# Gated linear attention and retention: both heads of a tile issued side by side on TensorE

## The chip, the cores and the metric

The kernel runs on one core of one Trainium2 chip. The metric is the device time of one execution in microseconds: 3158.46 as the median of three runs (3155.77 to 3163.26).

## What is computed

Two transformer-like blocks run one after the other on a sequence of 512 tokens, width 1024, two layers each. The change lies in the second block. There each layer projects its input once, splits the projection among four mixers (HGRN, gated linear attention or GLA, RWKV-7, retention; 256 columns each, four heads each), joins them, projects again, normalises and runs a feed-forward part (dense in layer 0, eight experts in layer 1). The parts that matter, from the reference:

```python
def _chunked_gated_linear(q, k, v, log_f):          # HGRN and GLA
    def step(state, inp):
        ...
        scores = jnp.einsum('bhik,bhjk,bhijk->bhij', qi, ki, decay)
        out = (jnp.einsum('bhij,bhjv->bhiv', scores, vi)
               + jnp.einsum('bhik,bhkv->bhiv', qi * jnp.exp(cum), state))
        ...
def _retention_chunkwise(q, k, v, log_gamma):       # retention
    def step(state, inp):
        ...
        scores = jnp.einsum('bhik,bhjk->bhij', qi, ki) * intra
        out = (jnp.einsum('bhij,bhjv->bhiv', scores, vi)
               + jnp.einsum('bhik,bhkv->bhiv', qi * q_dec[..., None], state))
```

The kernel computes the same sums without the carried state, as masked products over all 512 tokens: a token looks at every earlier one with the decay between the two.

## The kernel before

Activations of the second block lie with features on the 128 partitions and the 512 tokens along the free axis. A tile of 128 partitions holds two heads of 64 values. Keys are 64 wide in HGRN and retention (two heads on a tile), 32 wide in GLA (four heads on a tile). Work is written as Python generators, one for each mixer core. `weave` runs several of them together: each `yield` gives a share of a stated total, and the one that is least far along is continued. What is traced in that order goes to a scheduler, which fixes the order of each engine's queue when the program is built: an instruction is queued when its inputs and its buffers are there by the scheduler's own clock, earlier traced ones first.

The end of `mixers` weaves three times per layer: the two RWKV pairs with the HGRN and GLA projections; then the two HGRN cores `H(0)` and `H(1)` with the retention projection; then the GLA core, the retention core and the first half (`ph1`) of the output projection. Nothing else changes around these stages.

`linear_core` is the HGRN core (`nh` = 2 heads of 64 rows, called twice) and the GLA core (`nh` = 4 heads of 32 rows, called once). It runs nine levels. In the first seven, TensorE makes scores of all heads into an `sc` bank (`sc<-lE,lxk`), and VectorE copies them under a mask into one table per head, `dg[h]` (`ldg` in the profile, line 1897). The last two levels leave `a` and `b` (`lqk`), which cover the pairs of different 128-token blocks. Then comes the part that the change rewrites (lines 1902 to 1923): for each pair `m` of heads and each head `u` of it, two score matmuls of 128 columns into an `sc` bank and a copy on ScalarE (line 1910, to `o2`), two of 256 columns into another `sc` bank and a copy (line 1914, to `o1`), and ten value matmuls (64 columns of values as weights, 128 tokens moving) into half of the bank `op` (tag `av`). Both copies are named `lof`. A head's keys are a slice of rows of the array, a head's values a slice of its columns.

`ret_core` does the four retention heads, two on each tile `i`. For a head it loads a decay table of 512 columns (`ret`, line 1964); then for each of four blocks of keys it makes the scores of 512, 384, 256 or 128 queries into an `sc` bank, multiplies them with the table on VectorE (line 1970, to `tmp`), and adds the product with the values to half of the bank `op`.

Float32 matmuls on these lines go through the helper `mm` (line 1521), so the profile shows all of them under L1521; the tiles tell them apart. Projections use three float32r matmuls for one product (lines 406 to 408) with 512 or 256 columns.

PSUM has eight banks of 512 float32 columns, two for each of the tags `mm`, `sc`, `tp` and `av`. SBUF tiles of 128 x 512 are taken from one pool, tag `C`, with 47 buffers; `tmp` has 6 of its own. All loads go through SP's queue in order.

Of the kernel before, what the change touches and what calls it, by code (L numbers as in the profile page):

```python
# [19 lines left out]
P = 128  # L20
D = 1024
S = 512
# [15 lines left out]
V = 1.2  # L38
# [276 lines left out]
class K:  # L315
# [88 lines left out]
    def mm3(self, out, lh, ll, rh, rl, first, last):  # L404
        mm = self.nc.tensor.matmul
        mm(out, lh, rh, start=first, stop=False)  # L406
        mm(out, lh, rl, start=False, stop=False)  # L407
        mm(out, ll, rh, start=False, stop=last)  # L408
# [1109 lines left out]
        return o  # L1518

    def mm(self, out, lhsT, rhs, start=True, stop=True):  # L1520
        self.nc.tensor.matmul(out, lhsT, rhs, start=start, stop=stop)  # L1521

    def sigmoid(self, out, ps, hb=None, n=P):
        nc = self.nc
# [298 lines left out]
    def linear_core(self, Q, Kk, Pf, nh, V, gs, gname, m0):  # L1823

        nc = self.nc
        kd = P // nh
        X = self.c("lx")
        nc.gpsimd.memset(X, 0.0)  # L1830
        q = lambda x, t: x[:, t * P:(t + 1) * P]
        bc4 = lambda m: m.unsqueeze(1).to_broadcast([P, 4, P])
        v4 = lambda x: x.rearrange("p (t c) -> p t c", c=P)
        rr = [slice(kd * h, kd * h + kd) for h in range(nh)]
        dg = self.cs(nh, "ldg")

        qk = self.c("lqk")
        nc.gpsimd.tensor_mul(qk, Q, Kk)
        dp = self.bank("sc")
        for t in range(4):  # L1840
            self.mm(dp[:, t * nh:(t + 1) * nh], q(qk, t), self.heads[nh])
        dc = self.xp.tile([P, 16], F32, name="ldc", tag="ldc", bufs=2)[:, :4 * nh]
        nc.scalar.copy(dc, dp[:, :4 * nh])
        dv = dc.rearrange("p (t h) -> p t h", h=nh)
        for h in range(nh):
            nc.gpsimd.tensor_mul(v4(dg[h]), bc4(self.ident), dv[:, :, h:h + 1].to_broadcast([P, 4, P]))
        yield 0.5

        xk = [self.c("lxk") for _ in range(2)]
        ng = nh // 2  # L1850
        E = [[self.c("lE") for _ in range(ng)] for _ in range(2)]
        for b in range(2):
            nc.gpsimd.memset(xk[b], 0.0)
            for g in range(ng):
                nc.gpsimd.memset(E[b][g], 0.0)
        nt = 4 // ng
        top = []
        for n in range(9):
            s = 1 << n
            lv = lambda x: x.rearrange("p (b s) -> p b s", s=2 * s)  # L1860
            e = self.c("le")
            x = self.c("lqk") if n > 6 else xk[n % 2]
            self.act(lv(e)[:, :, s:], lv(Pf)[:, :, s:], AF.Exp)
            self.act(lv(e)[:, :, :s], lv(X)[:, :, :s], AF.Exp)
            nc.vector.tensor_mul(lv(x)[:, :, :s], lv(Kk)[:, :, :s], lv(e)[:, :, :s])
            if n > 6:
                nc.vector.tensor_mul(lv(x)[:, :, s:], lv(Q)[:, :, s:], lv(e)[:, :, s:])
                top.append(x)
            else:
                for g in range(ng):  # L1870
                    ts = slice(g * nt * P, (g + 1) * nt * P)
                    ev = E[n % 2][g].rearrange("p (t h b s) -> p t h b s", h=nh, t=nt, s=s)
                    half = lambda y: y[:, ts].rearrange("p (t b s) -> p t b s", t=nt, s=2 * s)[:, :, :, s:]
                    if g in EA[nh]:
                        nc.vector.tensor_mul(half(e), half(Q), half(e))
                    for h in range(nh):
                        if g in EA[nh]:
                            self.act(ev[:, :, h], half(e), AF.Identity, scale=self.heads[nh][:, h:h + 1])
                        else:
                            nc.vector.tensor_mul(ev[rr[h], :, h], half(Q)[rr[h]], half(e)[rr[h]])  # L1880
            if n < 8:
                nb = S // (2 * s)
                pv, xv = lv(Pf), lv(X)
                nc.gpsimd.tensor_add(xv[:, :, :s], xv[:, :, :s], pv[:, :, 2 * s - 1:2 * s].to_broadcast([P, nb, s]))
                nc.gpsimd.tensor_add(pv[:, :, s:], pv[:, :, s:], pv[:, :, s - 1:s].to_broadcast([P, nb, s]))
            if n > 6:
                continue
            mask = self.lvt(n).rearrange("p (b s) -> p b s", s=2 * s)[:, :, s:].unsqueeze(1)
            for g in range(ng):
                ps = self.bank("sc")  # L1890
                w = 64 * nh
                for t in range(nt):
                    self.mm(ps[:, t * w:(t + 1) * w], q(x, g * nt + t), E[n % 2][g][:, t * w:(t + 1) * w])
                pv = ps.rearrange("p (t h b s) -> p t h b s", h=nh, t=nt, s=s)
                for h in range(nh):
                    dst = dg[h][:, g * nt * P:(g + 1) * nt * P]
                    nc.vector.copy_predicated(dst.rearrange("p (t b s) -> p t b s", t=nt, s=2 * s)[:, :, :, s:],
                                              mask.to_broadcast([P, nt, 64 // s, s]), pv[:, :, h])
                yield 0.9
        a, b = top  # L1900
        offs = {(0, 1): (1, 0), (0, 2): (0, 0), (0, 3): (0, 1), (1, 2): (0, 2), (1, 3): (0, 3), (2, 3): (1, 1)}
        for m in range(nh // 2):
            op = self.bank("av")
            for u in range(2):
                h = 2 * m + u
                o1, o2 = self.c("lof"), self.c("lof")
                ps = self.bank("sc")
                self.mm(ps[:, 0:128], q(a, 0)[rr[h]], q(a, 1)[rr[h]])
                self.mm(ps[:, 128:256], q(a, 2)[rr[h]], q(a, 3)[rr[h]])
                nc.scalar.copy(o2[:, 0:256], ps[:, 0:256])  # L1910
                ps = self.bank("sc")
                self.mm(ps[:, 0:256], q(b, 0)[rr[h]], b[rr[h], 256:512])
                self.mm(ps[:, 256:512], q(b, 1)[rr[h]], b[rr[h], 256:512])
                nc.scalar.copy(o1, ps)
                v, h0 = V[m]
                ov = slice(64 * u, 64 * u + 64)
                for t in range(4):
                    o = q(op, t)[ov]
                    for j in range(t):
                        w, f = offs[j, t]  # L1920
                        self.mm(o, v(j, 64 * (h0 + u), 64), q((o1, o2)[w], f), j == 0, False)
                    self.mm(o, v(t, 64 * (h0 + u), 64), q(dg[h], t), t == 0, True)
                yield 3.0
            sq = self.c("lsq")
            self.act(sq, op, AF.Square)
            vp = self.bank("tp")
            self.mm(vp, self.blk, sq)
            self.rsqrt(sq, vp, "m_rms")
            nc.vector.scalar_tensor_tensor(sq, op, self.v2(gname), sq, op0=ALU.mult, op1=ALU.mult)
            nc.vector.tensor_mul(sq, sq, gs[m])  # L1930
            self.emit_y(m0 + m, sq, 0.5)
            yield 0.9
# [24 lines left out]
    def ret_core(self, d):  # L1957
        nc = self.nc
        for i in range(2):
            op = self.bank("av")  # L1960
            for u in range(2):
                h = 2 * i + u
                rr = slice(64 * u, 64 * u + 64)
                tab = self.load(self.aps["cst2"][:, 1154 + S * h:1154 + S * (h + 1)], "ret")
                for t in range(4):
                    n = S - t * P
                    ps = self.bank("sc")
                    self.mm(ps[:, :n], d["k"][i][rr, t * P:(t + 1) * P], d["q"][i][rr, t * P:])
                    s = self.tmp()
                    nc.vector.tensor_mul(s[:, :n], ps[:, :n], tab[:, :n])  # L1970
                    self.mm(op[rr, t * P:], d["v"][0](t, 64 * h, 64), s[:, :n], t == 0, t == 3)
                    yield 1.0
            o = self.c("gn")
            nc.scalar.copy(o, op)
            n, rs = self.group_norm(o, "m_ln")
            nc.vector.tensor_mul(n, n, rs)
            nc.vector.tensor_mul(n, n, d["g"][i])
            self.emit_y(6 + i, n, 0.5)
            yield 1.8
# [22 lines left out]
```

## Time and profile before

| | |
|---|---|
| median of three runs | 3158.46 us |
| lowest, highest | 3155.77, 3163.26 us |
| the profiled execution | 3172.64 us, its span 3170.8 us |
| TensorE matmul busy | 3013.7 us (95% of the span) |
| TensorE weight loads | 2454.5 us (77%) |
| VectorE, ScalarE, GpSimd | 1889.4, 1316.5, 355.8 us (60%, 42%, 11%) |
| mean granted TensorE clock | 0.97 |

The profile is of one execution, taken by the hardware. PE is TensorE's matmuls, PEld its weight loads, which overlap them; DVE is VectorE, ACT ScalarE, POOL GpSimd, SP the queue that issues loads. `sc<-lqk 64*128 64x256` reads: written to a tile named `sc`, read from `lqk`, 64 rows by 128 columns of the array, moving data of 64 partitions by 256 columns. The end of a matmul is modelled and reaches into the next one, so what an instruction costs is read from start to start. The layers of the second block begin their weaves of the linear cores at about 1440 and 2274 us of the span.

### The profile page before, as it was taken

How to read it: one execution, taken by the hardware profiler on the slowest of the kernel's cores; microseconds unless marked ns; L12 is line 12 of the kernel's file. 1: busy time of each engine (PE TensorE's matmuls, PEld its weight loads, DVE VectorE, ACT ScalarE, POOL GpSimd, SP SyncE). 2: the span in 40 equal slices, each digit the busy share in tenths (PEclk: the TensorE clock that was granted, in tenths of full speed). 3: DMA queues.
4: the chain of work that ended last, by engine and by line, in shares of the span. 5: the costliest groups of instructions: out<-in, count | busy, mean ns of one | idle time of the engine just before them, and what ended most of it. 6: DMA issues, size and time to landing. Idle time of an engine off the chain costs nothing. (4 is left out here: it accounts for less than half of the span.)

```text
span 3170.8 us, 46930 instructions
## 1 busy us (share of the span) xinstructions
PE 3013.7 (95%) x18729; PEld 2454.5 (77%) x18729; DVE 1889.4 (60%) x3318; ACT 1316.5 (42%) x2257; POOL 355.8 (11%) x377
## 2 busy tenths in 40 slices
PE   7999999999999999998999999999999799999997
PEld 5688888877878888786657888778775599999983
DVE  6676554657745566636554333555556677777775
ACT  3534333335433333424333222343353366666652
POOL 2220000211100001004210000100222200000021
PEclk9999999999999999999999999999999899999997
DMA  5322124242221433210202323421112278777782
GB/s 181 105 79 80 61 66 146 84 146 77 74 87 47 136 103 111 72 42 24 90 21 94 98 95 94 133 89 42 34 47 81 80 235 264 261 251 258 248 282 93
DMA packets 116534, 365.69 MB, mean 115 GB/s; under 512 B 13584, under 2 KB 16784, under 8 KB 116304
## 3 DMA queue, kind: packets, MB, share of 16 engines
q1 hardware_dynamic: 113424, 353.13, 34.2%
q0 software_dynamic: 2880, 9.44, 0.9%
q8 instruction: 150, 2.46, 0.3%
q14 instruction: 80, 0.66, 0.1%
HBM read 344.83 MB, written 17.69 MB: 114 GB/s over the span
## 5 line engine op out<-in xcount | busy, mean ns | idle before, releaser
L399 DVE TENSOR_TENSOR wl<-wr,wh 128x1024 fp32r<-128x1024 f32 (+1 forms) x574 | 698.3, 1225 | 520.2 <-ACT wh L395 508.2
L395 ACT CAST wh<-wr 128x1024 fp32r<-128x1024 f32 (+1 forms) x574 | 594.3, 1045 | 744.2 <-PE mm L407 355.4
L406 PE MATMUL mm<-hh,wh 128*128 128x512 f32 (+1 forms) x1616 | 651.4, 403 | 0.2
L407 PE MATMUL mm<-hl,wh 128*128 128x512 f32 (+1 forms) x1616 | 646.6, 400 | 0.0
L408 PE MATMUL mm<-hh,wl 128*128 128x512 f32 (+1 forms) x1616 | 642.8, 398 | 2.0 <-DVE wl L399 2.0
L406 PEld LDWEIGHTS mm<-hh,wh 128*128 128x128 f32 (+1 forms) x1616 | 306.9, 190 | 73.9 <-issue 6.3
L408 PEld LDWEIGHTS mm<-hh,wl 128*128 128x128 f32 (+1 forms) x1616 | 306.0, 189 | 74.5 <-issue 4.7
L407 PEld LDWEIGHTS mm<-hl,wh 128*128 128x128 f32 (+1 forms) x1616 | 307.0, 190 | 69.8 <-issue 6.2
L1266 PE MATMUL mm<-xgT,wh 128*128 128x320 f32 x704 | 218.5, 310 | 0.0
L1266 PE MATMUL sc<-xgT,wh 128*128 128x320 f32 x704 | 218.2, 310 | 0.1
L1267 PE MATMUL mm<-xgT,wl 128*128 128x256 f32 x704 | 198.1, 281 | 3.5 <-DVE wl L399 3.5
L1267 PE MATMUL sc<-xgT,wl 128*128 128x256 f32 x704 | 197.9, 281 | 0.0
L1267 PEld LDWEIGHTS mm<-xgT,wl 128*128 128x128 f32 x704 | 133.3, 189 | 5.9 <-DVE wl L399 5.6
L1266 PEld LDWEIGHTS mm<-xgT,wh 128*128 128x128 f32 x704 | 132.6, 188 | 1.2 <-DVE xgT L1245 0.4
L1266 PEld LDWEIGHTS sc<-xgT,wh 128*128 128x128 f32 x704 | 132.8, 189 | 0.3 <-DVE tmp L1272 0.3
L1267 PEld LDWEIGHTS sc<-xgT,wl 128*128 128x128 f32 x704 | 132.7, 188 | 0.0
L439 POOL TENSOR_TENSOR rs<-rs,mhalf 128x1 f32<-128x1 f32 x36 | 29.7, 825 | 905.1 <-DVE rs L438 790.7
L406 PE MATMUL mm<-wh,hh 128*128 128x256 f32 x448 | 129.6, 289 | 0.6 <-DVE sgv L754 0.6
L408 PE MATMUL mm<-wh,hl 128*128 128x256 f32 x448 | 128.4, 287 | 0.0
L407 PE MATMUL mm<-wl,hh 128*128 128x256 f32 x448 | 128.4, 287 | 0.0
L728 DVE TENSOR_REDUCE mn<-sc 128x1 f32<-128x512 f32 x64 | 44.1, 689 | 86.1 <-PE sc L725 85.9
L1521 PE MATMUL sc<-lE,lxk 128*128 128x128 f32 (+1 forms) x336 | 65.3, 338 | 25.4 <-ACT lE L355 11.6
(552 smaller groups left out, 5741.2 us busy)
## 6 DMA issues: line engine op xcount, KB each, us to landing
wr<-mgu SPq DMA_DIRECT2D x176, 512.0 KB, 4.8
wr<-w SPq DMA_DIRECT2D x172, 512.0 KB, 3.7
wr<-md SPq DMA_DIRECT2D x88, 512.0 KB, 4.5
wr<-fgu SPq DMA_DIRECT2D x44, 512.0 KB, 3.7
wr<-wo SPq DMA_DIRECT2D x32, 512.0 KB, 3.8
wr<-wbr SPq DMA_DIRECT2D x24, 512.0 KB, 3.7
row<-rows SPq DMA_DIRECT2D x40, 256.0 KB, 5.4
wr<-fd SPq DMA_DIRECT2D x20, 512.0 KB, 3.6
```

What stands on the lines that cost most here:

```text
L395: nc.scalar.copy(hi[:, :n], raw[:, :n])
L399: nc.vector.tensor_sub(lo[:, :n], raw[:, :n], hi[:, :n].bitcast(F32))
L406: mm(out, lh, rh, start=first, stop=False)
L407: mm(out, lh, rl, start=False, stop=False)
L408: mm(out, ll, rh, start=False, stop=last)
L439: self.nc.gpsimd.tensor_tensor(out, out, self.mhalf, op=ALU.pow)
L728: nc.vector.tensor_reduce(mx[u][:, a:a + 1], sc, axis=AX.X, op=ALU.min)
L1266: mm(o[i][:, :2 * CAP], wh, x[:, k, :2 * CAP], start=k == 0, stop=False)
L1267: mm(o[i][:, :256], wl, x[:, k, :256], start=False, stop=k == KT - 1)
L1521: self.nc.tensor.matmul(out, lhsT, rhs, start=start, stop=stop)
```

## The change

A helper `turns` issues one matmul for each of the two heads in turn and ties every one after the first (by issue order, not by a wait) behind the first, which is that of head `u` = 1. `linear_core` now makes, for a pair of heads, the 128-column scores of both into the two `sc` banks in turns, copies both, makes the 256-column scores of both into the two `tp` banks in turns, copies both, and after a `yield` makes the values of both in turns into the two halves of one `av` bank. Per pair it uses four `lof` buffers. `ret_core` loads both tables of a tile first; `weigh(t)` makes the scores of both heads into both `sc` banks and multiplies both; the scores of step `t + 1` are issued ahead of the values of step `t`. The count of matmuls, copies, multiplications and loads is the same, and so are the totals of the `yield` shares. No constant changes.

```diff
--- before.py
+++ after.py
@@ -1518,7 +1518,17 @@
         return o
 
     def mm(self, out, lhsT, rhs, start=True, stop=True):
-        self.nc.tensor.matmul(out, lhsT, rhs, start=start, stop=stop)
+        return self.nc.tensor.matmul(out, lhsT, rhs, start=start, stop=stop)
+
+    def turns(self, f, xs):
+
+
+        first = None
+        for x in xs:
+            for u in (1, 0):
+                with self.tc.issue_after(first) if first else nullcontext():
+                    i = f(u, x)
+                first = first or i.ins
 
     def sigmoid(self, out, ps, hb=None, n=P):
         nc = self.nc
@@ -1900,27 +1910,29 @@
         a, b = top
         offs = {(0, 1): (1, 0), (0, 2): (0, 0), (0, 3): (0, 1), (1, 2): (0, 2), (1, 3): (0, 3), (2, 3): (1, 1)}
         for m in range(nh // 2):
+            rows = [rr[2 * m + u] for u in range(2)]
+            o1, o2 = self.cs(2, "lof"), self.cs(2, "lof")
+            ps = [self.bank("sc") for _ in range(2)]
+            self.turns(lambda u, z: self.mm(q(ps[u], z), q(a, 2 * z)[rows[u]], q(a, 2 * z + 1)[rows[u]]), range(2))
+            for u in (1, 0):
+                nc.scalar.copy(o2[u][:, 0:256], ps[u][:, 0:256])
+            pb = [self.bank("tp") for _ in range(2)]
+            self.turns(lambda u, z: self.mm(pb[u][:, 256 * z:256 * z + 256], q(b, z)[rows[u]], b[rows[u], 256:512]),
+                       range(2))
+            for u in (1, 0):
+                nc.scalar.copy(o1[u], pb[u])
+            yield 3.0
             op = self.bank("av")
-            for u in range(2):
-                h = 2 * m + u
-                o1, o2 = self.c("lof"), self.c("lof")
-                ps = self.bank("sc")
-                self.mm(ps[:, 0:128], q(a, 0)[rr[h]], q(a, 1)[rr[h]])
-                self.mm(ps[:, 128:256], q(a, 2)[rr[h]], q(a, 3)[rr[h]])
-                nc.scalar.copy(o2[:, 0:256], ps[:, 0:256])
-                ps = self.bank("sc")
-                self.mm(ps[:, 0:256], q(b, 0)[rr[h]], b[rr[h], 256:512])
-                self.mm(ps[:, 256:512], q(b, 1)[rr[h]], b[rr[h], 256:512])
-                nc.scalar.copy(o1, ps)
-                v, h0 = V[m]
-                ov = slice(64 * u, 64 * u + 64)
-                for t in range(4):
-                    o = q(op, t)[ov]
-                    for j in range(t):
-                        w, f = offs[j, t]
-                        self.mm(o, v(j, 64 * (h0 + u), 64), q((o1, o2)[w], f), j == 0, False)
-                    self.mm(o, v(t, 64 * (h0 + u), 64), q(dg[h], t), t == 0, True)
-                yield 3.0
+            v, h0 = V[m]
+
+            def value(u, tj):
+                t, j = tj
+                w, f = offs[j, t] if j < t else (2, t)
+                return self.mm(q(op, t)[64 * u:64 * u + 64], v(j, 64 * (h0 + u), 64), q((o1[u], o2[u], dg[2 * m + u])[w], f),
+                               j == 0, j == t)
+
+            self.turns(value, [(t, j) for t in range(4) for j in range(t + 1)])
+            yield 3.0
             sq = self.c("lsq")
             self.act(sq, op, AF.Square)
             vp = self.bank("tp")
@@ -1958,18 +1970,27 @@
         nc = self.nc
         for i in range(2):
             op = self.bank("av")
-            for u in range(2):
-                h = 2 * i + u
-                rr = slice(64 * u, 64 * u + 64)
-                tab = self.load(self.aps["cst2"][:, 1154 + S * h:1154 + S * (h + 1)], "ret")
-                for t in range(4):
-                    n = S - t * P
-                    ps = self.bank("sc")
-                    self.mm(ps[:, :n], d["k"][i][rr, t * P:(t + 1) * P], d["q"][i][rr, t * P:])
-                    s = self.tmp()
-                    nc.vector.tensor_mul(s[:, :n], ps[:, :n], tab[:, :n])
-                    self.mm(op[rr, t * P:], d["v"][0](t, 64 * h, 64), s[:, :n], t == 0, t == 3)
-                    yield 1.0
+            rr = [slice(64 * u, 64 * u + 64) for u in range(2)]
+            tab = [self.load(self.aps["cst2"][:, 1154 + S * h:1154 + S * (h + 1)], "ret") for h in (2 * i, 2 * i + 1)]
+
+            def weigh(t):
+                n = S - t * P
+                ps = [self.bank("sc") for _ in range(2)]
+                self.turns(lambda u, x: self.mm(ps[u][:, :n], d["k"][i][rr[u], t * P:(t + 1) * P],
+                                                d["q"][i][rr[u], t * P:]), range(1))
+                out = [self.tmp() for _ in range(2)]
+                for u in range(2):
+                    nc.vector.tensor_mul(out[u][:, :n], ps[u][:, :n], tab[u][:, :n])
+                return out
+
+            s = weigh(0)
+            yield 1.0
+            for t in range(4):
+                x, s = s, weigh(t + 1) if t < 3 else None
+                yield 1.0
+                self.turns(lambda u, _: self.mm(op[rr[u], t * P:], d["v"][0](t, 64 * (2 * i + u), 64),
+                                                x[u][:, :S - t * P], t == 0, t == 3), range(1))
+                yield 0.75
             o = self.c("gn")
             nc.scalar.copy(o, op)
             n, rs = self.group_norm(o, "m_ln")
```

## Rows read from the trace of the kernel before

**Rows 1.** Page, section 1: busy us, share of the span, instructions.
```profile
PE 3013.7 (95%) x18729; PEld 2454.5 (77%) x18729; DVE 1889.4 (60%) x3318; ACT 1316.5 (42%) x2257; POOL 355.8 (11%) x377
```

**Rows 2.** Stretches, layer 0: length, busy PE PEld DVE ACT POOL (x), clock, DMA.
```profile
1440.00:1500.00 60.00, 48.33 (x260) 37.70 (x259) 45.91 (x76) 32.53 (x77) 37.08 (x48) 0.94 0.09 27
1500.00:1540.00 40.00, 39.70 (x238) 31.62 (x238) 12.46 (x17) 15.31 (x25) 0.00 (x0) 1.00 0.14 42
...
1563.00:1601.00 38.00, 31.46 (x113) 17.73 (x111) 33.53 (x105) 13.97 (x41) 10.40 (x14) 1.00 0.14 42
1601.00:1641.00 40.00, 38.75 (x174) 21.88 (x173) 16.12 (x30) 14.80 (x27) 1.43 (x2) 1.00 0.10 34
```

**Rows 3.** Order of time, PE, B2: start, us, engine, line, operation, tiles, shape.
```profile
1605.47 1.13 PE L1521 MATMUL sc<-lqk 32*128 32x256 f32 x4
1606.53 0.43 PE L1521 MATMUL av<-lof,vt 128*64 128x128 f32 x2
...
1607.11 1.12 PE L1521 MATMUL sc<-rx 64*128 64x512 f32 x2
1608.17 0.65 PE L1521 MATMUL av<-lof,vt 128*64 128x128 f32 x4
...
1608.87 0.82 PE L1521 MATMUL av<-lof,vt 128*64 128x128 f32 x6
1609.53 0.38 PE L1521 MATMUL av<-ldg,vt 128*64 128x128 f32 x2
1609.84 0.71 PE L1521 MATMUL sc<-lqk 32*128 32x128 f32 x4
1610.47 0.43 PE L1521 MATMUL av<-ldg,vt 128*64 128x128 f32 x2
...
1611.27 1.07 PE L1521 MATMUL av<-tmp,vt 128*64 128x512 f32 x2
1612.27 1.13 PE L1521 MATMUL sc<-lqk 32*128 32x256 f32 x4
```

**Rows 4.** Order of time, PE, in A: scores of two heads that meet.
```profile
1502.97 1.13 PE L1521 MATMUL sc<-lqk 64*128 64x256 f32 x8
1504.03 0.39 PE L406 MATMUL mm<-wh,hh 128*128 128x256 f32 x1
```

**Rows 5.** Order of time, PE, RWKV output, where two halves alternate.
```profile
1422.56 0.28 PE L1521 MATMUL av<-SB,W 128*64 128x128 f32 x1
1422.57 0.27 PE L1521 MATMUL av<-SB,vT 128*64 128x128 f32 x1
1422.67 0.27 PE L1521 MATMUL av<-SB,W 128*64 128x128 f32 x1
```

**Rows 6.** A stretch of 0.03 us, instructions on `ST` alone: PE, PEld.
```profile
1402.21:1402.24 0.03, 0.02 (x2) 0.02 (x2) 0.00 (x0) 0.00 (x0) 1.00 0.00 0
```

**Rows 7.** Order of time, PE, the function `full` of the RWKV code.
```profile
1401.36 0.93 PE L1521 MATMUL sc<-e,a 64*128 64x128 f32 x6
...
1402.48 1.16 PE L1521 MATMUL sc<-e,a 64*128 64x128 f32 x10
```

**Rows 8.** Instructions on `lof`, ACT: ns min/median/max, first and last start.
```profile
L1910 ACT COPY lof<-sc x16: 358/372/378, 1487.3 to 2459.1; 128x256 f32<-128x256 f32 x16
L1914 ACT COPY lof<-sc x16: 585/585/586, 1489.3 to 2462.0; 128x512 f32<-128x512 f32 x16
```

**Rows 9.** Waits of PE, 1538 to 1645: us in total, times, longest.
```profile
PE sc L1521 <- DVE ldg L1897: 3.1, 5, 1.1
```

**Rows 10.** Order of time, DVE: the copies that empty one such bank.
```profile
1569.35 1.31 DVE L1897 COPY_PREDICATED ldg<-msk,sc 128x128 f32<-128x128 uint8 x4
```

**Rows 11.** Waits of SP's queue, 1440 to 1660: us in total, times, longest.
```profile
SPq L371 <- PE sc L1521: 31.1, 1, 31.1
```

**Rows 12.** Order of time, SP's queue.
```profile
1542.15 4.73 SPq L371 DMA_DIRECT2D H<-hd  x8
...
1564.07 31.99 SPq L371 DMA_DIRECT2D ret<-cst  x2
```

## The prediction

> **What bounds the kernel now.** I read the page first: TensorE is busy for 95% of a span of 3170.8 us, the other engines for 60% and less [rows 1]. A busy TensorE is only a hint, so the second view was the table of stretches around the code that changes; layer 0 is shown [rows 2], and layer 1 runs the same stages again. Per layer there are three places. *A*, 1440 to 1540: two HGRN cores and the retention projections; in its first 60 us TensorE is busy for 48.3, in its last 40 for 39.7. *B1*, 1563 to 1601: the levels of the GLA core with the first retention tile; VectorE is busy for 33.5 of 38 us, TensorE for 31.5. *B2*, 1601 to 1641: the last part of the GLA core (all four heads) with the second retention tile; TensorE 38.8 of 40, VectorE 16.1. So B2 and the end of A are TensorE's, B1 is shared by VectorE and TensorE. The granted clock is 1.00 in all of them but the first 60 us of A (0.94), so the durations read there need no correction.
>
> The third view, the order of time on TensorE in B2, prices the work [rows 3]. The kernel issues float32 matmuls there, and each shows as two instructions (two matmuls of scores are a row of x4). Start to start, six value instructions of 128 columns take 1609.53 - 1608.87 = 0.66, so 0.11 us each, with half of the array's columns empty. One GLA head takes 0.63 (scores of 128 columns, 1609.84 to 1610.47), 1.06 (scores of 256 columns, 1605.47 to 1606.53), and for its 20 value instructions 0.58 (1606.53 to 1607.11) and 1.67 (1608.17 to 1609.84): 3.94 us. A retention step of 512 columns takes 1.06 for the scores and 1.00 for the values (1611.27 to 1612.27). Two instructions of 512 are worth 8 x 0.11 = 0.88, so 0.12 to 0.18 of each bout is the change of array shape and the first weight load. A retention head has four steps of 512, 384, 256 and 128 columns: 1280 columns are 20 x 0.11 = 2.2 for scores, as much for values, and eight bouts at 0.15 make 1.2: 5.6 us.
>
> **The change part by part.** It adds and removes no arithmetic. What it does is put two heads that sit in different halves of the array next to each other in TensorE's queue.
>
> *Do two halves run at once?* Three places of the trace show it. By rows: where the scores of two HGRN heads happen to meet, four instructions of 256 columns and four of 128 are done in 1.06 us (1502.97 to 1504.03), which is what the four of 256 take alone [rows 4, 3]. By columns: in the RWKV output two instructions of 128 columns start within 0.01 us of each other, and the next two 0.11 later [rows 5]. A single pair of matmuls, alone between other shapes: within 0.03 us two of its instructions are already running [rows 6]. I therefore take the cost of a pair as that of one head.
>
> *Ceiling.* Per layer: A has four heads, 4 x 3.94 = 15.8, less about 0.6 that rows 4 already overlap, so 15.2, half of which is 7.6. B2 has four GLA heads, 15.8, half 7.9, and two retention heads, half of 11.2: 5.6. B1 has the other two retention heads: 5.6. In all 26.7 us a layer, 53 in two.
>
> *What of it lies on the path.* B2 is TensorE's, with no gap in the rows; I take 0.8 of 13.5 = 10.8. The missing fifth is for two things. Values now wait for four evictions instead of two (0.37 and 0.58 each [rows 8]); the second head's copy is late by up to 0.58 per pair, hidden by the other stream's matmuls while there are any, 2.3 us a layer if not. And the order is fixed when the program is scheduled: the helper ties every matmul behind the first of the later head, but if one head's copy is ready earlier, that head runs ahead unpaired by up to 0.58 us, and the other follows unpaired. In A the first HGRN head lies where TensorE waits anyway (11.7 of 60 us idle), so I take two thirds of 7.6: 5.0.
>
> *B1 and the score banks.* There are two `sc` banks. Before, a retention step took one and a GLA level the other, and already TensorE waited for VectorE to empty one: five times, 3.1 us in all, up to 1.1 [rows 9]. `weigh` takes both. The GLA scores queued behind a retention pair then wait until both multiplications are through, and the pair waits for two banks. This wait is not in the trace; bounds: zero when the banks fall free anyway, 1.1 us for each of eight steps (four pairs, waited for on either side) = 8.8 by the row. I take 5.1, nearer the middle, since VectorE, which empties both, is 88% busy there. Against a gain of 5.6 this leaves 0.5. VectorE's multiplications and ScalarE's evictions are as many as before. The Trainium skill's "TensorEngine Tiling (Array Packing)", section PSUM Bottleneck, says that tiling speeds up TensorE but not the emptying of PSUM; by that rule B1 gives nothing at all, and the sum below would end 1 us higher.
>
> *Loads.* The table of the second head is asked for right after the first, so on SP's queue it passes eight loads of `H`, four of `row` and two of weights. Its issue takes about 0.6 us (eight like it took 4.73 [rows 12]), covered by the projections that run meanwhile. But it needs a buffer of the pool `C`, and one such load of a later head waited 31.1 us for TensorE to give one back, holding up what is behind it on SP [rows 11]. If that happened to the first tile's second table, the loads of `H` would be late by up to 22 us (1542.15, when they began, to 1564.07, when the old load was issued [rows 12]). I take 0, since the buffer was free when the old load came up, and keep the 22 us for the range. Four `lof` buffers instead of two come at a time when the level tiles have been given back: 0 taken, at worst one eviction late per pair (0.58).
>
> *Pacing.* The shares that the streams are given for the weave stay: retention 2 x (8 x 1.0 + 1.8) = 19.6 before, 2 x (1.0 + 4 x 1.75 + 1.8) = 19.6 after; GLA 26.9 both times. Scores of the next step now come ahead of the values of this one, so VectorE's multiplication no longer stands between two matmuls of one step; I give that nothing.
>
> *Sum.* 5.0 + 0.5 + 10.8 = 16.3 us a layer, 32.6 in two. The profiled execution took 3172.6 (span 3170.8 and 1.8 around it), 14.2 over the median of the runs; the gain is taken off both. From the median: 3158.5 - 32.6 = 3125.9.
>
> **The rivals.**
>
> *Passes one after the other.* If the two instructions of one head stand together in the queue and starts are strictly in order, a lone pair takes three passes instead of two, a group of two pairs five of eight, the values 21 of 40. Savings are then 25% for retention, 37% for scores, 47% for values: B2 15.8 x 0.43 + 11.2 x 0.25 = 9.6, of which 0.8 is 7.7; A 15.2 x 0.43 x 2/3 = 4.3; B1 2.8 - 5.1 = -2.3. Per layer 9.7, in two 19.4: 3139. Against it speak rows 6: two starts within 0.03 us. The Trainium skill states the condition in "TensorE: Matmul & The Clock Gate", Part 3, on what overlaps: matmuls are "strict FIFO, no reordering". By that rule the time is this rival's, unless the two passes alternate in the queue as well.
>
> *The turns are not taken.* In `full` of the RWKV code the two heads alternate in the source too, and yet 6 and 10 instructions took 0.93 and 1.16 us, 0.13 each, as one head after the other would [rows 7]: the order written is lost when one head is ready first. The helper is there against that, but it holds only the start. With half of the gain of A and B2 and none in B1, about 16 in all: 3143.
>
> *Everything shows.* The idle time of A and the waits of B1 are covered: 53 us, 3105.
>
> *Slower: the banks.* The place is every `weigh`, 16 in two layers, the mechanism that it holds or awaits both `sc` banks while GLA's levels and scores queue behind it on TensorE. The price for one is at most two level scores emptied one after the other, 1.06 us of scores (four instructions of 256 columns [rows 3]) and 1.31 of copies [rows 10] each, 4.7 in all; 16 are 75 us, 42 more than the gain: 3201. It decides from 32.6 / 16 = 2.0 us of added idle time per step. Against it: eight of the 16 are in B2, where no level runs, and TensorE has projections to do.
>
> **How the numbers follow.** Forecast 3126: 0.58. Passes in turn, 3139: 0.10. Turns lost, 3143: 0.12. Everything shows, 3105: 0.13. Banks: 0.07. Range: from 3104 (everything shows) to 3149: the two smaller gains, with 6 us for a load that waits or a schedule that shifts. About 0.2%, 6 us, is what a measurement here can tell from no change. The forecast, the two smaller gains and the full one lie beyond that; from the turns lost and the forecast I give 0.06 to less than 6 us: faster 0.86, same 0.07, slower 0.07.
>
> **What would show it.** In the order of time of B2, `sc<-lqk` rows of x8 in about 0.65 and 1.06 us, the values of a pair (40 instructions) in about 2.3, a retention pair of 512 columns (x4) in about 1.0 where two took 2.1; B2 from 40 to about 29 us, A shorter by 5, B1 as long as before with longer waits of TensorE for VectorE. If a lone retention pair takes 1.4 us, the first rival holds; if value rows come in runs of one head at 0.11, the second; if TensorE's idle time in B1 grows by more than 8 us a layer, the banks decide. The prediction is wrong if TensorE's saved time turns up as idle time in B2: then the chain from scores to copy to values was the bound beneath it.

## The result and the profile after

The changed kernel takes 3112.35 us (median of four runs, 3109.97 to 3123.69); the kernel before, 3160.86 in four runs beside them. The ratio is 0.9844 (95% interval 0.9823 to 0.9864): 48.5 us off, where 32.6 were forecast. The time lies inside the range, and the direction is right; the gain is half as large again, close to the ceiling of 53. A second series of six runs, beside eleven of the kernel before, gave 3116.44 against 3166.51, 0.9835 (0.9811 to 0.9860): 50 us.

One view shows most of it. The stretches are now cut at marks that every kernel has: A begins with the first scores of the HGRN levels, B0 with the decays of GLA, B1 with GLA's first level scores, B2 with its last; B2 ends with the last normalisation sum of the retention. Stretches of the kernel after, columns as in [rows 2]; A, B0, B1, B2 of layer 0, then B0, B1, B2 of layer 1:

```profile
1428.90:1517.00 88.10, 78.66 (x486) 63.27 (x484) 54.98 (x91) 45.88 (x100) 36.81 (x48) 0.94 0.12 37
1517.00:1548.00 31.00, 27.98 (x86) 17.70 (x85) 17.08 (x23) 10.90 (x18) 11.58 (x15) 0.78 0.55 185
1548.00:1583.80 35.80, 32.15 (x111) 20.82 (x111) 30.36 (x100) 14.62 (x42) 7.25 (x11) 0.86 0.06 17
1583.80:1607.50 23.70, 23.11 (x163) 13.01 (x161) 14.50 (x28) 12.15 (x23) 0.69 (x2) 1.00 0.14 45
2331.80:2356.50 24.70, 21.67 (x85) 14.09 (x85) 17.22 (x23) 10.75 (x18) 12.04 (x15) 1.00 0.70 229
2356.50:2389.10 32.60, 28.86 (x111) 19.03 (x111) 29.93 (x100) 14.64 (x42) 7.24 (x11) 0.95 0.07 21
2389.10:2414.40 25.30, 24.72 (x162) 14.05 (x161) 14.48 (x28) 12.15 (x23) 0.71 (x2) 0.93 0.14 42
```

The kernel before, B1 and B2 of layer 0 at the same marks:

```profile
1567.20:1600.80 33.60, 29.08 (x102) 16.30 (x103) 29.24 (x99) 12.67 (x38) 6.52 (x10) 1.00 0.05 17
1600.80:1640.90 40.10, 38.85 (x174) 21.88 (x173) 16.22 (x30) 14.80 (x27) 1.43 (x2) 1.00 0.10 34
```

B2 was 40.1 us and is 23.7. It stays TensorE's: 23.1 of 23.7 us busy. B1 has TensorE and VectorE almost level. The granted clock, third column from the end, matters too: B0 takes 31.0 us in layer 0 at a mean clock of 0.78 and 24.7 in layer 1 at 1.00, with the same instructions. The clock has two levels, 2.4 GHz (1.00) and 1.2 GHz (half). So each length stands below with the time that it spent at half clock, 2 x (1 - clock) x length (clock unrounded), in brackets; us, layer 0 and layer 1:

| kernel | A | B1 | B2 |
|---|---|---|---|
| before | 96.5 (7), 97.1 (10) | 33.6 (0), 33.6 (0) | 40.1 (0), 40.1 (0) |
| after | 88.2 (10), 88.1 (10) | 35.8 (10), 32.6 (3) | 23.7 (0), 25.3 (3) |
| after, second series | 88.2 (10), 87.7 (10) | 35.7 (10), 35.8 (10) | 23.7 (0), 23.7 (0) |
| linear cores only | 88.2 (10), 87.7 (10) | 33.6 (0), 33.6 (0) | 35.7 (7), 35.7 (7) |
| retention only | 98.3 (14), 97.8 (14) | 32.6 (3), 35.8 (10) | 34.3 (3), 34.3 (3) |
| head after head | 91.9 (10), 90.5 (7) | 34.1 (7), 32.6 (3) | 29.2 (3), 29.3 (3) |
| same rows | 88.8 (10), 88.3 (10) | 34.6 (7), 35.7 (10) | 32.3 (14), 29.1 (7) |
| `tp` and `sc` for retention | 87.0 (7), 87.5 (10) | 30.0 (3), 30.0 (0) | 24.8 (0), 24.8 (0) |

Second series against before: -22.6 us in layer 0, -23.6 in layer 1, together 46.2, where the medians are 50 apart. The two executions profiled are 62.4 us apart (spans of 3170.8 and 3108.4 us): B0 has 3.5 of the rest, and the other 13 lie outside these stages.

The order of time on TensorE in B2, as in [rows 3] (kernel after):

```profile
1586.91 1.12 PE L1521 MATMUL sc<-rx 64*128 64x512 f32 x2
1587.96 1.13 PE L1521 MATMUL tp<-lqk 32*128 32x256 f32 x8
1589.03 1.12 PE L1521 MATMUL sc<-rx 64*128 64x512 f32 x2
1590.08 0.44 PE L1521 MATMUL av<-lof,vt 128*64 128x128 f32 x4
...
1591.88 0.39 PE L1521 MATMUL av<-ldg,vt 128*64 128x128 f32 x4
1592.19 0.91 PE L1521 MATMUL sc<-rx 64*128 64x384 f32 x2
...
1594.93 1.08 PE L1521 MATMUL av<-tmp,vt 128*64 128x512 f32 x4
1595.94 0.87 PE L1521 MATMUL sc<-rx 64*128 64x256 f32 x4
```

Start to start: the 256-column scores of two heads (x8) take 1.07 us, what one head's took. Of the 40 value instructions of two heads, 36 stand together here and take 2.11 (1590.08 to 1592.19), 0.059 each where [rows 3] had 0.11; the other four ran at 1584.09. Retention's values of two heads (x4 of 512 columns) take 1.01, where one head's took 1.00. But the retention scores of 512 columns are two rows of x2 with other work between them, 1.05 us each, and those of 384 columns are two rows as well. They did not pair. Those of 256 stand together (x4), but the second head starts 0.18 us late, and the two take 0.80 where one head's took 0.63.

Waits of TensorE from 1515 to 1612 (us in total, times, longest), for [rows 9]:

```profile
PE sc L1521 <- DVE tmp L1983: 2.8, 2, 1.9
PE sc L1521 <- DVE lE L1890: 2.0, 1, 2.0
PE mm L406 <- ACT yh L417: 1.5, 3, 0.9
PE sc L1521 <- DVE ldg L1907: 0.8, 2, 0.4
```

A level's scores now wait for retention's multiplication (`tmp`), 2.8 us, where they waited for the levels' own copies (`ldg`), 3.1 before and 0.8 now. The bank wait changed its name and about kept its size (3.6 for 3.1).

SP's queue for [rows 11, 12], in order of time:

```profile
1519.69 0.85 SPq L371 DMA_DIRECT2D ret<-cst  x2
1520.87 4.95 SPq L371 DMA_DIRECT2D H<-hd  x8
...
1578.68 1.27 SPq L371 DMA_DIRECT2D ret<-cst  x2
```

Both tables of the first tile are asked for together and `H` follows 0.3 us after: the late load of the first tile's second table did not happen.

### The profile page after: what moved, and what is told of

The parts are those of the page before. It is cut to its first block, busy times and chain, and to the rows that moved or that the text cites. A ratio compares the mean times of both kernels' runs of the same rounds, so it can differ in the third digit from the quotient of the medians.

```text
span 3121.9 us, 46921 instructions
## 1 busy us (share of the span) xinstructions
PE 2969.5 (95%) x18729; PEld 2426.4 (78%) x18729; DVE 1881.3 (60%) x3318; ACT 1314.5 (42%) x2257; POOL 357.0 (11%) x377
## 5 line engine op out<-in xcount | busy, mean ns | idle before, releaser
L355 ACT ACTIVATE tmp<-mm,hvec 128x512 f32<-128x512 f32 x72 | 49.4, 686 | 96.1 <-PE mm L408 96.1
```

The lines of the kernel that those rows point to most:

```text
L355: i = self.nc.scalar.activation(out, src, f, **kw)
```

## The experiments

**One half of the change alone.** The linear cores as changed with the retention of before, and the reverse. The diff of each is the one hunk of the change put back.

> The HGRN and GLA cores of the change, the retention core of the kernel before. If the gain is the halves of the array running at once, this keeps what A gave in the traces (8 to 9 us a layer) and the GLA part of B2 (half of 15.8, and some changes of array shape): 16 to 18 us a layer, 32 to 36 us under the kernel before. If retention carried it, under 20.

> The retention core of the change, the HGRN and GLA cores of the kernel before. The value pairs of retention ran at once in the trace (four instructions of 512 columns in 1.01 us), most of its scores did not (512 and 384 columns came apart). So half of the values, 2.7 us a head pair and 5.4 a layer, and little of the scores: 10 to 14 us under the kernel before if nothing is lost in B1; 4 to 8 if the score banks cost what the prediction took.

Measured: linear cores only 3131.65 us against 3160.70, 0.9911 (0.9890 to 0.9933), 29 us; retention only 3153.07, 0.9971 (0.9957 to 0.9984), 8 us. The first is less than expected, the second lies in the lower of its two cases, and their sum, 37, is about 12 short of the whole. The stretch B2 of layer 0, first of the one kernel, then of the other:

```profile
1579.30:1615.00 35.70, 32.49 (x175) 19.13 (x173) 16.23 (x30) 14.90 (x28) 1.44 (x2) 0.90 0.12 38
```

```profile
1592.00:1626.20 34.20, 32.11 (x162) 19.95 (x161) 14.60 (x28) 12.66 (x23) 0.68 (x2) 0.95 0.10 32
```

The kernel before has no half-clock time in B2. By an estimate, at full clock these would be about 32.3 and 32.6 us (half of the half-clock time taken off, since TensorE fills the stage), 7.8 and 7.5 less than before; 15.3 together, next to 16.4 with both. So in work the halves add up, and about 10 us (two layers, 3.4 and 1.7) of the missing 12 are clock that each half alone gives back in B2. The two are not alike, though: with the linear cores alone, B2 keeps its 19 projection instructions, and with the retention alone it has 9, the other ten having gone to B1. In A all of the gain is the linear cores', none the retention's.

**Turns against head after head.** Same banks, same buffers, but all matmuls of one head before those of the other.

```diff
-        for x in xs:
-            for u in (1, 0):
+        for u in (1, 0):
+            for x in xs:
...
-                first = first or i.ins
+                first = i.ins
```

> The changed kernel with the loops of the helper exchanged and each matmul tied to the one before: all of one head, then all of the other, still in one group. Lone pairs of retention stay as they are. If two halves at once are the gain, the linear cores lose 20 x 0.11 = 2.2 us of values and up to 1.3 of scores in each of 8 pairs: 18 to 28 us slower than the changed kernel, that is 20 to 30 under the kernel before. If grouping is the gain (fewer changes of array shape), it stays within 6 us of the changed kernel.

Measured: 3133.09 us, 0.9921 (0.9899 to 0.9942), 21 to 22 us less gain than the changed kernel's, within what was expected. Order of time in B2:

```profile
1590.82 1.14 PE L1521 MATMUL tp<-lqk 32*128 32x256 f32 x8
1591.88 1.12 PE L1521 MATMUL sc<-rx 64*128 64x512 f32 x2
1592.94 0.43 PE L1521 MATMUL av<-lof,vt 128*64 128x128 f32 x2
...
1594.08 0.71 PE L1521 MATMUL av<-lof,vt 128*64 128x128 f32 x5
1594.52 0.32 PE L1521 MATMUL av<-ldg,vt 128*64 128x128 f32 x1
1594.63 0.27 PE L1521 MATMUL av<-lof,vt 128*64 128x128 f32 x1
1594.68 0.32 PE L1521 MATMUL av<-ldg,vt 128*64 128x128 f32 x2
1594.79 0.27 PE L1521 MATMUL av<-lof,vt 128*64 128x128 f32 x1
1594.84 0.27 PE L1521 MATMUL av<-ldg,vt 128*64 128x128 f32 x1
...
1596.54 0.38 PE L1521 MATMUL av<-ldg,vt 128*64 128x128 f32 x2
1596.85 0.91 PE L1521 MATMUL sc<-rx 64*128 64x384 f32 x2
```

The values (38 of the 40 stand together here) take 3.91 us instead of 2.11, so the turns are worth 1.8 us per pair. The scores of 256 columns (x8) still take 1.06: four instructions of one head behind four of the other overlap as well as turns do, as [rows 4] had shown. Turns matter for the long groups.

The rows from 1594.08 on show why. The first head's values end with six `lof` and two `ldg`, and the second head's begin with two `ldg`. The `ldg` at 1594.52 is the second head's first, and it starts while three of the first head have still to start: the sixth `lof` (1594.63) and two `ldg` (one of the two in the row of 1594.68, and that of 1594.84). So an instruction for the other half of the array started here ahead of three that stand before it in the queue. That is enough for four and four; of a long group it reaches the last few only.

**Two halves of the array, or a better queue?** Every queue as in the changed kernel, but the scores of both heads read the rows of the second head; so two neighbours in TensorE's queue use the same half.

```diff
-            self.turns(lambda u, z: self.mm(q(ps[u], z), q(a, 2 * z)[rows[u]], q(a, 2 * z + 1)[rows[u]]), range(2))
+            self.turns(lambda u, z: self.mm(q(ps[u], z), q(a, 2 * z)[rows[1]], q(a, 2 * z + 1)[rows[1]]), range(2))
...
-                self.turns(lambda u, x: self.mm(ps[u][:, :n], d["k"][i][rr[u], t * P:(t + 1) * P],
-                                                d["q"][i][rr[u], t * P:]), range(1))
+                self.turns(lambda u, x: self.mm(ps[u][:, :n], d["k"][i][rr[1], t * P:(t + 1) * P],
+                                                d["q"][i][rr[1], t * P:]), range(1))
```

> The changed kernel, but the scores of both heads read the rows of the second head, so that they sit in the same half of the array: the first head's scores are left out and the second's made twice, with as many instructions, in the same order on every engine. If the gain of the scores is two halves at once, this is slower than the changed kernel by what was paired: 0.86 us for 256 columns in each of 8 pairs, 0.44 for 128 in about half of them, and two or three of the retention steps a layer: 9 to 12 us. If it comes from issuing them together, there is no difference.

Measured: 3131.61 us, 0.9913 (0.9895 to 0.9930), some 20 us slower than the changed kernel, more than expected. Order of time in B2:

```profile
1584.01 1.99 PE L1521 MATMUL tp<-lqk 32*128 32x256 f32 x8
1585.92 1.97 PE L1521 MATMUL sc<-rx 64*128 64x512 f32 x2
1587.82 0.69 PE L1521 MATMUL av<-lof,vt 128*64 128x128 f32 x4
```

The eight scores now take 1.91 us for 1.07: the gain of these scores is the second half of the array and nothing else. Right behind them the granted clock falls from 2.4 to 1.2 GHz, though TensorE was busy all through those 1.91 us: the mean is 0.54 from 1585.92 to 1587.82, where two retention scores, as many as before and as wide, take 1.90 for 1.05. B2 has 14 and 7 us of half clock in its two layers, about 10 us of the 20 when half of it counts as lost.

**Why the retention scores came apart.** Three kernels with other banks, and the changed kernel once more on the same chip.

```diff
-                ps = [self.bank("sc") for _ in range(2)]
+                ps = [self.bank("tp"), self.bank("sc")]
```

This line of `weigh` is the first of them. The second changes in the same way the line of `linear_core` that takes the banks of the 128-column scores; the third takes two `tp` banks in `weigh` and leaves `linear_core` alone.

> The changed kernel itself, a second time, so that the three kernels with other score banks have it on the same chip. Every theory: 3110 to 3116 us, 45 to 51 under before; its two retention scores of 512 columns still appear as two rows of x2 of 1.05 us each.

> The retention scores take one bank of tag tp and one of tag sc instead of two of sc. Theory: their pairs came apart because each matmul goes into its own sc bank, the two fall free at different times, and the tie orders the pair without holding it together; per layer this costs two times 1.05 (512 columns), two times 0.84 (384) and about 0.4 (128), some 4.2 us. With a bank of either tag they stand together as x4: 1.05 us at 512 columns, and the kernel is 8 us (4 to 12) faster than the changed one: about 3104. Rival 1: in the stage with the GLA levels VectorE is the bound and the pairs there bring nothing; only 1.9 us a layer show, 4 us in all. Rival 2: the tp banks are what the 256-column scores and the norms wait for, and taking one gives it all back: no difference within 3 us, or slower.

> As the kernel with one tp and one sc bank for the retention scores, and the 128-column scores of the linear cores take tp and sc as well. Theory: the same cause acts on these pairs, where some came apart (x4 of 0.61 and 0.64 one after the other); putting them together is worth up to 0.6 us per pair that came apart, two or three per layer: 2 to 3 us below the other kernel, 10 us below the changed one (about 3101). Rival: the 256-column scores that follow need both tp banks, which now wait for one copy more; 0 to 5 us slower than the other kernel.

> The retention scores take both banks of tag tp, none of sc. Theory on the banks: the sc banks are left to the GLA levels, so the waits for a tmp multiplication before a level's scores (2.8 us in one layer) go, but in the last part the 256-column scores of GLA compete for tp. If the wait that took the place of the ldg wait costs time, this is 2 to 6 us faster than the changed kernel (3106 to 3110); if VectorE's work alone sets that stage, it is the same within 3 us; if both banks of one tag are again taken one at a time, the pairs come apart as before and nothing of the 4.2 us a layer is won.

Measured against 3166.51 of before: the changed kernel 3116.44, 0.9835 (0.9811 to 0.9860), at the upper edge of what was expected; `tp` and `sc` for retention 3100.72, 0.9784 (0.9762 to 0.9807); for both cores 3104.63, 0.9808 (0.9785 to 0.9830); `tp` alone 3112.12, 0.9837 (0.9818 to 0.9856). Order of time on TensorE in the first, in B0 (at half clock there) and in B2:

```profile
1528.68 1.06 PE L1521 MATMUL sc<-rx 64*128 64x512 f32 x1
1528.69 1.06 PE L1521 MATMUL tp<-rx 64*128 64x512 f32 x1
...
1586.67 0.59 PE L1521 MATMUL sc<-rx 64*128 64x384 f32 x1
1586.68 0.59 PE L1521 MATMUL tp<-rx 64*128 64x384 f32 x1
1587.10 0.48 PE L1521 MATMUL sc<-rx 64*128 64x384 f32 x1
1587.11 0.48 PE L1521 MATMUL tp<-rx 64*128 64x384 f32 x1
```

With two tags the name of the tile shows which head an instruction belongs to. The heads start in turn, 0.01 us apart, and two of 384 columns, one of each head, need 0.43 us (1586.67 to 1587.10), so the four need about 0.86 where two needed 0.84. In the program as built they do not stand in turn: the two instructions of one head come first, then the two of the other. Only one pair per layer is still apart (512 columns in B2, 0.73 and 1.06). Stretches B1 and B2 of layer 1:

```profile
2348.10:2378.10 30.00, 23.52 (x99) 14.93 (x100) 27.98 (x98) 13.56 (x41) 6.67 (x10) 1.00 0.08 22
2378.10:2402.90 24.80, 24.24 (x174) 14.17 (x172) 15.71 (x29) 13.41 (x25) 1.23 (x2) 1.00 0.13 43
```

B1 falls to 30.0 us, with VectorE busy for 28.0 of them. The theory holds in direction: the pairs stand together and the kernel is 16 us faster than the changed one, more than the 4 to 12 expected, and the two intervals do not meet. Rival 1 falls (B1 is 3.6 us shorter than before, with 18 projection instructions for 17), rival 2 as well. What the runs do not separate is how much of the 16 is the paired work and how much the clock: B1 had 10 us of half clock in the changed kernel and 0 to 3 here. Nor is all that B1 lost against the changed kernel a gain: nine of its 27 projection instructions are back in B2, so B1 and B2 together go from 59.4 to 54.8. `tp` and `sc` for the linear scores too adds nothing that can be told (the intervals overlap); in B2 of layer 0 its second pair of them came apart all the same. `tp` alone gives nothing that can be told (the intervals overlap): in B2 the 384-column scores are again apart, and the wait for `tmp` is there under another name:

```profile
1580.88 0.91 PE L1521 MATMUL tp<-rx 64*128 64x384 f32 x2 [1.41 <-DVE tmp L1983]
1582.13 0.91 PE L1521 MATMUL tp<-rx 64*128 64x384 f32 x2
```

The starts of the eight retention steps of a layer sum it up, the same in both layers. With two `sc` banks six steps have other work between the heads, in one the second head is 0.18 us late, and one is together (0.01). With two `tp` banks it is one, four (0.16 to 0.60 late) and three; with one bank of each, none, one (0.74) and seven. So two banks of one tag parted the heads in most steps, and one bank of each of two tags in one of eight; that this comes of the two banks falling free one after the other is argued. Pairing is not all: `tp` alone pairs more steps than the changed kernel, with no gain that can be told. In its B2 the 256-column scores of GLA's second pair, which take `tp` too, run one head after the other (eight in 1.91 us). The kernel with `tp` and `sc` for retention beats both kernels of this case.

**The clock in B1.** The retention scores of the first tile made twice, to give TensorE more to do there (12 of a layer's 16 added instructions run in B1, four in B0); in the changed kernel, and in the one with `tp` and `sc`.

```diff
-                                                d["q"][i][rr[u], t * P:]), range(1))
+                                                d["q"][i][rr[u], t * P:]), range(2 - i))
```

> The changed kernel with the retention scores of the first tile made twice into the same banks (the second time writes over the first), 32 TensorE instructions more, all beside the GLA levels. Question: the stage with the levels had 10.2 us at half clock in three of four layers profiled of the changed kernel, none in the kernel before. Theory: pairing leaves TensorE idle there while VectorE works, and the clock falls after that idle time; with 2560 columns more per layer (20 x 0.11 = 2.2 us in single file, 1.4 side by side) TensorE is as busy as before, the half clock goes from about 10 to 0 to 3.4 us, the stage from 35.7 to about 32, and the whole is 0 to 8 us faster than the changed kernel (about 3108 to 3116). Rival: the clock falls for another reason; the stage keeps its 10 us and grows by 1 to 2 us, the whole is 2 to 4 us slower than the changed kernel.

> The same doubling in the kernel that takes one tp and one sc bank for the retention scores. There the stage with the levels had 3.4 us and 0 us at half clock and took 30.0 us in both layers. Either theory: nothing to win, the stage stays at 30 to 31 us, the whole is the same within 4 us as that kernel (3100 to 3105); a longer stage would say that TensorE has become its bound.

Measured against 3158.45: 3118.72, 0.9884 (0.9863 to 0.9906), and 3100.43, 0.9828 (0.9802 to 0.9854). Stretches B1 and B2 of layer 0 of the first:

```profile
1537.50:1570.00 32.50, 32.50 (x124) 21.99 (x124) 29.10 (x98) 14.61 (x40) 5.91 (x9) 0.91 0.00 1
1570.00:1600.40 30.40, 27.77 (x161) 14.84 (x160) 14.73 (x30) 12.09 (x25) 1.29 (x2) 0.78 0.15 53
```

In B1 the theory looks right: more work, and yet 32.5 us for 35.7, with half-clock time down from 10 to 6 us (3 in layer 1). But B2 behind it now has 14 and 7 us of half clock and takes 30.4 and 28.3 for 23.7, and the forecast of a gain failed: the whole is 2 to 6 us slower than the changed kernel by its time, and more by its ratio (the changed kernel was not run beside it). The second kernel is no faster than without the doubling; its stages are within 1.3 us of it in B1 and B2, and its ratio is 0.9828 against 0.9784, the intervals just overlapping. The clock loss moved; what sets its place stays open.

## Why the prediction was right, and where its sizes were off

To see which work got cheaper, TensorE's time in a stage is summed by kind, start to next start, so that idle time lies with the instruction before it (layer 0; us):

| stage, kind | before | after, second series |
|---|---|---|
| A: scores and values of HGRN | 15.6 | 10.6 |
| A: projections; the rest | 59.1; 21.8 | 56.1; 21.6 |
| B1: scores; values of retention | 6.8; 4.6 | 7.2; 2.4 |
| B1: projections; the rest | 6.5 (17); 15.7 | 8.7 (27); 17.5 |
| B2: scores; values of GLA | 6.6; 10.3 | 4.3; 4.7 |
| B2: scores; values of retention | 5.9; 5.3 | 5.0; 2.6 |
| B2: projections; the rest | 8.2 (19); 3.8 | 3.8 (9); 3.3 |

*Two halves run at once* [rows 4 to 6]: right. Pairs cost what one head costs, for scores of 256 columns (1.07 us for 1.06), for values (2.11 for one head's 2.25), and for retention's values (1.01 for 1.00); same rows and head after head take the gain away.

*Passes one after the other* falls: lone pairs of values (x4) take 1.01 us, not 1.4. Its condition was met, since in the program as built the two instructions of one head stand together; what failed is its price, strict order of starts. In the rows with two tags the heads start in turn all the same, and head after head, one instruction started ahead of three that stood before it (1594.52). By the rule of the Trainium skill ("TensorE: Matmul & The Clock Gate", Part 3), that matmuls start in strict order, the time would have been 3139. These traces do not agree with it where two instructions use different halves of the array, and the measurement decides.

*The turns are not taken* holds for one kind of work that I had not set apart: the retention's scores, in six of eight steps a layer (of 512 and 384 columns two rows, 1.05 and 0.84 us each, that should have cost half), and some first scores of the linear cores. I had looked for the danger where a copy is ready early; the kernels with other banks point to the bank that is free early. The tie of the helper decided nothing: built without it, the program has the same queues on every engine.

*A*, 5.0 forecast: 8.3 to 9.4. The pairs themselves saved 5.0 (15.6 to 10.6), the forecast's number, but not for its reason: values went from 9.7 to 5.5 us, near half, and scores only from 6.0 to 5.0. The step that failed is the third that I took off for TensorE's idle time. That idle time was not fixed, and it shrank. Waits of TensorE in A, layer 0, the two longest before and then after (second series):

```profile
PE sc L1521 <- ACT lE L355: 8.2, 3, 5.0
PE sc L1521 <- POOL lqk L1838: 1.6, 1, 1.6
```

```profile
PE sc L1521 <- POOL lf L1895: 4.3, 1, 4.3
PE sc L1521 <- POOL lqk L1848: 1.7, 1, 1.7
```

All waits listed there are 11.6 us before and 9.1 after, 2.5 less. The likely reason, argued and not tested: the chain that TensorE waits for contains matmuls of the other core, and those finish earlier.

*B1 and the score banks*, 0.5 forecast (5.6 of gain, 5.1 of waits): 2.2 longer in layer 0, 1.0 shorter in layer 1; in the second series 2.1 and 2.2 longer. Of the gain, only the values' half came (4.6 to 2.4); the scores did not pair. Of the cost, the added bank waits are about nil. What ate the rest were two costs that I had not listed: ten projection instructions that came from B2 (2.2 us), and up to 10 us of half clock in a stage that had none before. The clock's part can be read from the changed kernel itself: 35.8 us with 10 us of half clock in layer 0, 32.6 with 3 in layer 1, the same instructions. By the rule of the Trainium skill's "TensorEngine Tiling (Array Packing)", section PSUM Bottleneck, B1 would have given nothing. The changed kernel agrees with that; the kernel with `tp` and `sc` doesn't, with 30.0 us for 33.6, and there VectorE, busy for 28.0 of 30.0, is indeed what is left.

*B2*, 10.8 of 13.5 forecast: 16.4 and 14.8. The pairs gave 11.5 (2.3 + 5.6 + 0.9 + 2.7), 0.85 of the ceiling for 0.8. The other 4.9 are mostly work that left the stage (4.4): ten of 19 projection instructions now run in B1, where they cost 2.2. I had bounded each stage by its own work and had not asked what would move between them. A sum over B1 and B2 is the safer term: 11.3 forecast, 14.2 in layer 0.

*Loads and `lof` buffers*: right for the first tile, nothing late. *Slower: the banks*: it needed 2.0 us per `weigh`; the rows show 2.8 us in two waits for the eight of a layer.

Why the whole came near the ceiling: per layer 22.6 and 23.6 where 16.3 were forecast, of 26.7. The forecast's discounts were for idle time in A (wrong, it shrank), for bank waits (wrong, they only changed places) and for B2's fifth (right in size). In part this is luck: in layer 0 the pairs gave 5.0, 1.8 and 11.5, so 18.3 of the 26.7, and the other 4.3 are idle time in A and work between the pairs, less what B1 lost.

Nor was 53 us a ceiling. The kernel with `tp` and `sc` is 66 us under the kernel before, and its A, B1 and B2 alone are 57 shorter in the two layers. The ceiling halved the pairs' own instructions and left out that idle time and projections beside them can get shorter too. It was also read a little low: the 0.58 and 1.67 us of [rows 3] for a head's values hold 18 of its 20 instructions, and the other two stand alone (for the next head the x2 at 1610.47, 0.37 us).

## What to carry to other kernels

When small matmuls of two heads can share the array, price the pair as one head, put their instructions in turns where groups are long (18 and more here; four and four overlapped without), and look in the trace for whether the pair stands together. If it doesn't, try banks for the two outputs from two different pools: here that put seven of eight steps together, where two banks of one pool left one to three, and a pair that is parted gains nothing. Bound the gain over neighbouring stages together, since work moves into the room that is made. And look at the granted clock of each stretch before crediting or blaming an edit: here a stage of one kernel (B0) differs by 6 us between layers with the same instructions.

## What was not expected of the hardware

- Work taken from TensorE came back in part as half-clock time nearby. B1 had none in the kernel before and in the one with the linear cores alone; every kernel with retention in pairs had 3 to 10 us of it, but for one layer of the one with `tp` and `sc`. Doing more work there moved it into B2 (14 and 7 us). In the same-rows kernel the clock fell while TensorE was busy without a gap. What decides was not found.
- Six executions of the changed kernel on one chip lie between 3098.5 us (mean granted clock 0.974) and 3120.7 (0.967). A term of 5 us can't be read from one execution's total; it can from a stage at the same clock.
- Four float32 value instructions of two heads, 512 columns each, need 1.01 us together, as two of one head do (column halves), and eight scores of 256 columns need 1.07, as four of one head do (row halves): two halves of the array really worked at the same time.
- The starts do not keep the order of the queue where two instructions use different halves: one started ahead of three that stood before it (1594.52, head after head).
